# A hybrid decoder layer on one core: LayerNorm, pointwise convolution and a quarter of the first half of the output projection placed inside the prompt's stick-breaking attention

## The chip, the core and the metric

One core of a Trainium2 chip runs the whole program in one launch. The metric is the device time of one execution in microseconds, lower is better. Engines are named as the profile names them: PE (TensorE matmuls), PEld (its weight loads), DVE (VectorE), ACT (ScalarE), POOL (GpSimd), SP (SyncE, which here only issues DMAs).

## What is computed

One layer of a decoder trunk, for a prompt of 2048 tokens and for 32 sample tokens (8 sequences of 4). The parts that matter here:

```python
z = rms_norm(x) @ w_in                       # split into the inputs and gates of four groups
y_c = silu(layer_norm(depthwise_conv(u))) @ w_pw + b_pw     # group A, 512 channels
y_p = per_group_linear(causal_mean(u) - u) * scale          # group B (pooling), 512 channels
y_s = stick_breaking_attention(q, k, v)      # group C, 8 heads x 64, strictly causal
y_m = cross_attention(mq, mem)               # group D, 4 heads x 128
mix = concat(y_c*silu(cg), y_p*silu(pg), y_s*silu(sg), y_m*silu(mg))   # 2048 channels
out = x + rms_norm(mix @ w_out)              # w_out is 2048 x 1024
y   = rms_norm(out)
# attention of one head: z = q.k/8 + bias, beta = sigmoid(z), gamma = sigmoid(-z)
# a[q,k] = beta[q,k] * product of gamma[q,j] over the keys j between k and q
```

## The kernel before, in words

Everything is float32; a matmul that has to be exact splits both factors into a rounded float32r part and a remainder (names ending in `hi` and `lo`) and sums three products, hi·hi, hi·lo, lo·hi. Intermediate results that a later stage reads go through DRAM: `mixd` holds the gated outputs of all four groups, 16 blocks of 128 channels by 2080 tokens (blocks 0 to 3 convolution, 4 to 7 pooling, 8 to 11 attention, 12 to 15 cross-attention).

The program has three stages one after the other. Instructions on PE stand in the order in which the code issues them; the other engines' instructions are put into an order by a scheduler when the program is built, and each engine works through its own queue in that order.

1. **Projection and sample attention** (about the first 1516 us): `z`, the depthwise convolution, pooling, cross-attention and the 32 sample tokens' attention over the paged cache. The change doesn't touch it.

2. **The prompt's attention**, generator `sb_prompt` (L1158), 16 blocks (4 head pairs by 4 blocks of 512 queries), each going over its key blocks from the diagonal back to the first. A *step* is one call of `score` (L1183): four matmuls into a PSUM tile `S` of two banks (L1189), two sigmoids on ACT (`gam` L1195, `be` L1197), then, two steps late, on DVE a `tensor_tensor_scan` along the keys that forms the running product `E` (L1209; L1206 on the diagonal), and on POOL the product `be*E` (L1222). Six steps later `turn` (L1227) transposes `be` on PE into a PSUM tile with tag `AT` of which there are two (L1233), which DVE or ACT copies out (L1237 on the diagonal; elsewhere every third on DVE, L1243, the others on ACT, L1241); two steps after that `values` (L1246) multiplies with V into `av` (L1253). The scan takes `max(gamma*previous, data1)`, where `data1` is 0, or on the diagonal 0 with a triangle of 1; that tile, `ZM` (L1165), fills one PSUM bank, and every scan reads from it. PSUM is full: `S` twice two banks, `AT` twice one, `av` one, `ZM` one.

   `sb_prompt` yields twice per step with a cost; the loop around it (L1633 on) spends that cost on other work: first `side_work` (cross-attention of the sample tokens, the end of their attention, five tiles of `w_out`), and from the 300th yield of some 340 on `conv_work`, one piece per yield.

   `conv_post` (L1310) is that other work: LayerNorm, swish and pointwise convolution of group A, in eight blocks of 256 tokens. Per block: sums over channels on POOL, `center` (mean by a matmul with ones, L1334; four subtractions on DVE, L1337; squares on ACT, L1339), `scale` (variance by matmul, L1345; square root on ACT, L1347; reciprocal, L1348, and eight more operations on DVE, L1353 and L1357; sigmoids on ACT, L1356), `point` (four times twelve matmuls of 256 columns, L1374, gated and biased on DVE, L1377, and stored to `mixd`).

3. **The output projection.** For each of 17 token tiles (16 of the prompt, one of the samples) and each half `hf` of 512 output columns, 16 channel blocks by three products: 48 matmuls of 512 columns (L1619; 32 for the samples). `out_mix` (L1438) loads 8 channel blocks of `mixd` and splits them (ACT L1451, DVE L1453); `out_weights` (L1415) loads and splits `w_out`. `order` (L1599) lists half-tiles; those that hold the convolution's channels (half 0) come five tiles after the others, and the rest of `conv_post` (all but its first block) and the weights of the second half run between the matmuls of the first half. `out_keep` (L1458) copies the first half's results to `okeep` and sums their squares; `out_tile` (L1464) finishes a tile in the second half.

## Time and profile before

| | us |
|---|---|
| median of 3 runs | 2501.28 (2498.33 to 2506.47) |
| the profiled execution's own time | 2494.88 |
| its span, first to last instruction | 2493.2 |
| mean granted PE clock in it | 0.983 |
| first score matmul of the prompt's attention | 1516.4 |
| last matmul of it begins | 2046.2 |

The span and all times inside it come from one profiled execution. A row of the profile such as `L1209 DVE TENSOR_TENSOR_SCAN E<-gam,cr,ZM ... x192 | 235.8, 1267 | 5.5` is a group of instructions: source line, engine, operation, output and inputs by their names in the program, shapes, how many; then us busy in all, mean ns of one; then us for which the engine stood idle just before them, and what ended that. PE's matmuls are pipelined: an instruction's recorded length is longer than the distance to the next one, so PE's cost is read from starts or from counts per time, not from its busy share.

### The profile page before, as it was taken

To read this page: it belongs to the slowest core of one execution; us is meant where nothing else is said; L and a number is where in the kernel's file an instruction comes from. 1 tells how busy PE (TensorE), PEld (TensorE's weight loads), DVE (VectorE), ACT (ScalarE), POOL (GpSimd) and SP (SyncE) were. 2 spreads that over 40 slices of the span, in tenths; PEclk is the share of its full clock that TensorE was granted. 3 is DMA by queue.
4 is the path that set the end of the run, shared out by engine and by line. 5 is a ranking of instruction groups with operands and counts; after the bars stand their busy time and mean duration, and the time that the engine had idled before them with its cause. 6 is when DMAs were issued, how large, how long until landed. Compare 5 with 4: busy or idle time off the path is not lost. (4 is left out here: it accounts for less than half of the span.)

```text
span 2493.2 us, 42024 instructions
## 1 busy us (share of the span) xinstructions
PE 2331.7 (94%) x16154; PEld 1812.5 (73%) x16154; DVE 1695.1 (68%) x2402; ACT 1073.9 (43%) x1867; POOL 1231.6 (49%) x1330
## 2 busy tenths in 40 slices
PE   6998999999999999999999997898999879999998
PEld 6997878788888677777777774455555547887786
DVE  5442495969747663587877677899899966554554
ACT  5324224242442322223232343777888854444443
POOL 2543545455564555645555663567766742320221
PEclk9999999999999999999999998999999999999999
DMA  5688677777778899878877748434332116445664
GB/s 178 216 273 285 240 259 263 239 258 256 259 246 303 286 345 326 298 267 277 286 265 273 266 167 211 128 86 111 98 85 74 46 45 180 138 117 149 179 193 140
DMA packets 347554, 518.07 MB, mean 208 GB/s; under 512 B 26257, under 2 KB 250897, under 8 KB 330954
## 3 DMA queue, kind: packets, MB, share of 16 engines
q1 hardware_dynamic: 291978, 246.67, 33.4%
q0 software_dynamic: 55376, 268.72, 30.5%
q8 instruction: 127, 2.08, 0.3%
q14 instruction: 73, 0.60, 0.1%
HBM read 444.12 MB, written 71.81 MB: 207 GB/s over the span
## 5 line engine op out<-in xcount | busy, mean ns | idle before, releaser
L856 DVE STREAM_TRANSPOSE T<-kt 128x1024 f32<-128x1024 f32 x256 | 309.1, 1226 | 193.4 <-PE sSA L869 179.3
L823 POOL DMA_INDIRECT vt<-in_cache_v_dram,idv x256 | 250.8, 980 | 241.3 <-PE sO L908 179.5
L519 DVE SCALAR_TENSOR_TENSOR cacc<-U,par,cacc 128x512 f32<-128x512 f32 x480 | 358.9, 748 | 8.0
L1222 POOL TENSOR_TENSOR be<-be,E 128x512 f32<-128x512 f32 (+2 forms) x320 | 304.8, 955 | 117.8 <-DVE E L1209 64.6
L1209 DVE TENSOR_TENSOR_SCAN E<-gam,cr,ZM 128x513 f32<-128x513 f32 x192 | 235.8, 1267 | 5.5 <-POOL be L1222 4.1
L823 POOL DMA_INDIRECT kt<-in_cache_k_dram,idk x128 | 125.5, 981 | 228.1 <-DVE T L856 169.6
L1233 PEld LDWEIGHTS AT<-ident,be 128*128 128x128 f32 x1088 | 118.3, 142 | 158.4 <-DVE at L1243 27.7
L1619 PE MATMUL acc<-wohi,mh 128*128 128x512 f32 (+1 forms) x544 | 219.8, 404 | 6.6 <-ACT wohi L1432 6.6
L1619 PE MATMUL acc<-wolo,mh 128*128 128x512 f32 (+1 forms) x544 | 216.2, 397 | 0.0
L1195 ACT ACTIVATE gam<-S,nbias_bc 128x128 f32<-128x128 f32 (+1 forms) x224 | 177.3, 792 | 83.0 <-PE S L1189 48.4
L1619 PE MATMUL acc<-wohi,ml 128*128 128x512 f32 x512 | 203.5, 398 | 0.0
L1233 PE MATMUL AT<-ident,be 128*128 128x128 f32 x1088 | 163.8, 285 | 38.5 <-DVE at L1243 23.2
L1197 ACT ACTIVATE be<-S,bias_bc 128x128 f32<-128x128 f32 (+1 forms) x224 | 176.6, 788 | 0.0
L1189 PE MATMUL S<-kT,Q 128*128 128x512 f32 (+3 forms) x640 | 172.1, 392 | 1.5 <-DVE sg1sg L611 1.5
L1253 PE MATMUL av<-at,V 128*64 128x512 f32 (+3 forms) x640 | 154.9, 563 | 2.1 <-DVE sbo L1258 2.1
L869 PE MATMUL sSA<-T,W 128*32 128x128 f32 x4096 | 139.5, 277 | 14.1 <-DVE T L856 12.9
L1453 DVE TENSOR_TENSOR ml<-mr,mh 128x1024 fp32r<-128x1024 f32 (+1 forms) x65 | 82.8, 1274 | 95.8 <-ACT mh L1451 95.7
L869 PEld LDWEIGHTS sSA<-T,W 128*32 128x32 f32 x4096 | 105.0, 110 | 51.6 <-issue 45.5
L1483 POOL TENSOR_TENSOR oxt<-oxt,oy 128x1024 f32<-128x1024 f32 (+1 forms) x16 | 39.3, 2457 | 183.4 <-DVE oy L1478 162.6
L1619 PEld LDWEIGHTS acc<-wohi,mh 128*128 128x128 f32 (+1 forms) x544 | 101.9, 187 | 31.7 <-ACT wohi L1432 8.2
L908 PE MATMUL sO<-vt,saT 128*32 128x512 f32 x1024 | 122.0, 593 | 0.0
L1619 PEld LDWEIGHTS acc<-wolo,mh 128*128 128x128 f32 (+1 forms) x544 | 101.8, 187 | 24.8 <-DVE wolo L1433 0.9
(560 smaller groups left out, 6002.3 us busy)
## 6 DMA issues: line engine op xcount, KB each, us to landing
mr<-mixd SPq DMA_DIRECT2D x63, 512.0 KB
Q<-qd SPq DMA_DIRECT2D x64, 256.0 KB
xtp<-in_x_prompt_dram SPq DMA_DIRECT2D x16, 512.0 KB
kT<-kd SPq DMA_DIRECT2D x64, 128.0 KB
wor<-in_w_out_dram SPq DMA_DIRECT2D x32, 256.0 KB
oxt<-in_x_prompt_dram SPq DMA_DIRECT2D x16, 512.0 KB
out_dram<-oy SPq DMA_DIRECT2D x15, 512.0 KB
wr0mem<-in_w_mem_kv_dram SPq DMA_DIRECT2D x8, 512.0 KB
```

The source lines that it names most:

```text
L519: dve.scalar_tensor_tensor(out=ps, in0=U[:, a + k : a + k + H], scalar=wd[:, k : k + 1], in1=ps, op0=ALU.mult, op1=ALU.add)
L823: pool.indirect_dma_start(out=dst, out_offset=None, in_=rows, in_offset=bass.IndirectOffsetOnAxis(ap=idx, axis=0))
L856: dve.transpose(T[:, 2 * hh : 2 * hh + 2].rearrange("p s j t -> p (s j t)"), kt[:, 2 * hh : 2 * hh + 2].rearrange("p s j d -> p (s j d)"))
L869: pe.matmul(sSs[n][32 * g : 32 * g + 32, P * ml : P * (ml + 1)], lhsT=W[:, jj, :], rhs=T[:, :, jj, :], start=i == 0, stop=i == 3, tile_pos ...
L1189: pe.matmul(S[:, j, :n], lhsT=Q[hh][:, x, P * (q2 + j) : P * (q2 + j + 1)], rhs=KT[hp, hh, kc][:, :n], start=x == 0, stop=x == 1)
L1195: act.activation(out=ga[:, j0:j1, 512 - n : 512], in_=S[:, j0:j1, :n], func=AF.Sigmoid, bias=nbias_bc[:, h : h + 1], scale=-1.0)
L1197: act.activation(out=be[:, j0:j1, :n], in_=S[:, j0:j1, :n], func=AF.Sigmoid, bias=bias_bc[:, h : h + 1])
L1209: dve.tensor_tensor_scan(out=E[:, j][:, ::-1], data0=ga[:, j][:, ::-1], data1=ZM[:, 0:1].to_broadcast([P, 513]), initial=carry[hh, q2][:, ...
L1222: pool.tensor_tensor(out=be[:, j, :m], in0=be[:, j, :m], in1=E[:, j, 513 - n : 513 - n + m], op=ALU.mult)
L1233: pe.transpose(ap_[:, P * qt : P * (qt + 1)], A[hp, qb, kc, hh, qt][:, P * r : P * (r + 1)], ident)
L1253: pe.matmul(av[64 * hh : 64 * hh + 64, c], lhsT=V[:, 4 * kc + r, 64 * hh : 64 * hh + 64], rhs=ats.pop((hp, qb, kc, r, hh))[:, c], start=dg ...
L1619: pe.matmul(o[:rows], lhsT=m[i][:, k, :rows], rhs=W[hf, 8 * half + k][w], start=n0 + k == 0 and i == w == 0, stop=n0 + k == 15 and (i if t ...
```

## The change

- The tile of zeros and triangle shrinks to 129 columns of its PSUM bank (`ZX`), and columns 256 to 511 of the same bank become an accumulator. A scan on the diagonal that is longer than 128 becomes two: 128 columns with the triangle, then the rest with a zero that is broadcast and the first scan's last value as its start.
- `conv_post` becomes part of the side work: it follows the samples' work at once and is paced by the attention's cost (one piece per 1.25 units of it; the attention has about 362).
- New generator `early_out`, one piece per 4.2 units: for all 17 token tiles the pooling blocks 4 to 7 are multiplied with the first 512 output columns, in two passes of 256 columns, each pass twelve matmuls in two groups of six into the shared bank, then a copy on ACT; the result goes to DRAM (`okd`). Then it loads weights 8 to 11.
- The output stage works in quarters (4 channel blocks): three per tile in the first half, four in the second. `okeep` is filled from `okd` and the first half's sums are added to it. The weights of the second half are spread over the matmuls of the first; the queue of prepared tiles is five quarters of 256 KB instead of four halves of 512 KB; eight accumulators instead of six.

```diff
-PACE = 2.5
-OPACE = 1.15
-LAG = 5
+PACE = 1.6
+CPACE = 1.25
+EPACE = 4.2
+WPACE = 9.0
+SLATE = 8
+LAG = 3
-D1 = 6
-D2 = 12
-CSTART = 300
+D1 = 4
+D2 = 8
...
-        ZM = bps.tile([P, 512], F32, name="ZM", bufs=1)
-        act.copy(ZM, zm)
+        act.copy(ZX[:, : P + 1], zm)
+        zero = lambda n: ZX[:, 0:1].to_broadcast([P, n])
...
-                        dve.tensor_tensor_scan(out=E[:, j, 512 - n : 512][:, ::-1], data0=ga[:, j, 512 - n : 512][:, ::-1],
-                                               data1=ZM[:, 512 - n : 512][:, ::-1], initial=1.0, op0=ALU.mult, op1=ALU.max)
+                        dve.tensor_tensor_scan(out=E[:, j, 384:512][:, ::-1], data0=ga[:, j, 384:512][:, ::-1],
+                                               data1=ZX[:, 1 : P + 1][:, ::-1], initial=1.0, op0=ALU.mult, op1=ALU.max)
+                        if n > P:
+                            dve.tensor_tensor_scan(out=E[:, j, 512 - n : 384][:, ::-1],
+                                                   data0=ga[:, j, 512 - n : 384][:, ::-1], data1=zero(n - P),
+                                                   initial=E[:, j, 384:385], op0=ALU.mult, op1=ALU.max)
...
+    def out_products(o, hf, t, g, m, cols, first, last):
+        rows = P if t < 16 else 2 * NS
+        for k in range(4):
+            for i, w in ((0, 0), (0, 1), (1, 0)) if t < 16 else ((0, 0), (0, 1)):
+                pe.matmul(o[:rows], lhsT=m[i][:, k, :rows], rhs=W[hf, 4 * g + k][w][:, cols],
+                          start=first and k == i == w == 0, stop=last and k == 3 and (i if t < 16 else w) == 1)
+            yield
+    def early_out():
+        yield from out_weights(0, range(4, 8), opm, pool, True)
+        o = ZX[:, 256:512]
+        mix = {0: out_mix(0, 1, "e", pool)}
+        for t in range(17):
+            if t < 16:
+                mix[t + 1] = out_mix(t + 1, 1, "e", pool)
+            m = mix.pop(t)
+            rows = P if t < 16 else NS
+            ke = opm.tile([P, 512], F32, tag="ke", name=f"ke{t}", bufs=1)
+            for q in range(2):
+                cols = slice(256 * q, 256 * q + 256)
+                for k, _ in enumerate(out_products(o, 0, t, 1, m, cols, True, True)):
+                    if k % 2:
+                        yield
+                if t < 16:
+                    act.copy(ke[:, cols], o)
...
+            wq.dma_start(okd[t, :rows], ke[:rows])
+        yield
+        yield from out_weights(0, range(8, 12), opm, pool, True)
     def out_keep(t, o):
-        act.activation(out=okeep[:rows, t], in_=o[:rows], func=AF.Square, accum_out=ssk[:rows, t : t + 1])
-        dve.tensor_copy(okeep[:rows, t], o[:rows])
+        dve.tensor_tensor(out=okeep[:rows, t], in0=o[:rows], in1=okeep[:rows, t], op=ALU.add)
+        sq = op.tile([P, 512], BF16, tag="oksq", name=f"oksq{t}", bufs=1)
+        act.activation(out=sq[:rows], in_=okeep[:rows, t], func=AF.Square, accum_out=ssk[:rows, t : t + 1])
...
-    order = [(0, t, 1) for t in range(LAG)]
+    order = [(0, t, 2) for t in range(LAG)]
     for t in range(17):
-        order += [(0, t, 0)] + [(0, t + LAG, 1)] * (t + LAG < 17)
-    order += [(1, t, h) for t in [0, 1, 2, 16, *range(3, 16)] for h in range(2)]
+        order += [(0, t, 3), (0, t, 0)] + [(0, t + LAG, 2)] * (t + LAG < 17)
+    order += [(1, t, g) for t in [0, 1, 2, 16, *range(3, 16)] for g in range(4)]
...
+        if steps > SLATE:
+            sdue -= cost
+            while side is not None and sdue <= 0.0:
+                    sdue += next(side)
...
+        edue -= cost
+        while early is not None and edue <= 0.0:
+            edue += EPACE
+                next(early)
...
-    wts = out_weights(0, [*range(8 + NPRE, 16), *range(8)], lambda k: opw)
+    wts = out_weights(0, [*range(12, 16), *range(4)], opw, dve)
```

More of the change, by code (lines that the diff above doesn't have):

```diff
@@ L53 @@
 X0 = 8
-PACE0 = 1.5
 SEND = 0.97
@@ new lines, with prepare @@
+    order += [(1, t, g) for t in [0, 1, 2, 16, *range(3, 16)] for g in range(4)]
+    left_ = {}
+    for x in order:
+        left_[x[:2]] = left_.get(x[:2], 0) + 1
+    total_ = dict(left_)
+    mix, accs = {}, {}
+    def prepare(i):
+        for x in order[: i + 1]:
+            if x not in mix:
+                mix[x] = out_mix(x[1], x[2], f"{x[0]}_", dve if op else pool)
+                if x[0] == 0 and x[2] == 0:
+                    rows = P if x[1] < 16 else NS
+                    sp.dma_start(okeep[:rows, x[1]], okd[x[1], :rows])
@@ L1654 @@
-    for _ in side or ():
-        pass
-    bx.close()
-    for _ in range(early, NPRE):
-        next(first)
+                early = None
+        if "last" in flags and side is None and early is None:
+            if lead is None:
+                os_.close()
+                accp = oy.enter_context(tc.tile_pool(name="oacc", bufs=1, space=PSUM, side="left", reuse_waits="tile"))
+                prepare(1)
+                lead = out_part(order[0])
+            next(lead, None)
+    for g_ in (side, early):
+        for _ in g_ or ():
+            pass
@@ L1660 @@
+    bx.close()
+    if lead is None:
+        os_.close()
+        accp = oy.enter_context(tc.tile_pool(name="oacc", bufs=1, space=PSUM, side="left", reuse_waits="tile"))
+        prepare(1)
+        lead = out_part(order[0])
+    for _ in lead:
+        pass
     op = oy.enter_context(tc.tile_pool(name="op", bufs=2, side="right", reuse_waits="tile"))
[L1661 to L1662 removed]
@@ L1689 @@
-    other = other_work()
-    due, ope = 0.0, None
+    w1 = out_weights(1, range(16), op2, dve)
+    ope = None
+    due = 0.0
     for i, x in enumerate(order):
-        hf, t, half = x
+        hf = x[0]
         if hf and ope is None:
-            while "weights" not in flags:
-                next(other, 0)
+            for _ in w1:
+                pass
             ow.close()
```

191 lines of the change are left out of this document (71 added, 120 removed).

## The prediction

> **What bounds the kernel now.** I read the page first, then the busy times of three stretches, then the groups of instructions in them, then the waits.
>
> ```profile
> PE 2331.7 (94%) x16154; PEld 1812.5 (73%) x16154; DVE 1695.1 (68%) x2402; ACT 1073.9 (43%) x1867; POOL 1231.6 (49%) x1330
> ...
> PE acc L1619 14%; PE cz L1374 2%; DMA mr<-mixd 1%; PE av L1253 0%; PE AT L1233 0%; POOL slo L1359 0%; DMA mixd<-sbo 0%; DMA cgt<-gcd 0%; PE cm L1334 0%; PE cv L1345 0%; ACT mh L1451 0%; DVE cgt L1377 0%; PE S L1189 0%; ACT csg L1356 0%; DVE ml L1453 0%
> ```
>
> PE is 94% busy over the span, and the chain that ended last is made of the output projection's matmuls (`acc`). It only reaches back into the last fifth of the span, so it says nothing of the attention. The second view takes the span apart: body and drain of the prompt's attention, head and body of the output projection, then one head pair with side work, one without, and 100 us of nothing but output matmuls.
>
> ```profile
> core 0: us, PE busy (x) PEld busy (x) DVE busy (x) ACT busy (x) POOL busy (x), PEclk, DMA share, GB/s
> 1534.60:2018.30 483.70, 430.92 (x2447) 248.02 (x2443) 438.25 (x575) 375.83 (x571) 326.66 (x469) 0.99 0.34 90
> 2018.30:2047.00 28.70, 23.99 (x117) 12.39 (x115) 15.25 (x24) 15.43 (x28) 9.57 (x12) 0.94 0.08 23
> 2047.00:2070.00 23.00, 16.61 (x70) 12.94 (x71) 11.25 (x15) 8.74 (x12) 0.65 (x1) 0.78 0.59 177
> 2070.00:2482.90 412.90, 408.51 (x1927) 336.19 (x1926) 214.98 (x314) 172.33 (x316) 97.61 (x80) 1.00 0.54 158
> 1659.30:1786.40 127.10, 112.29 (x631) 65.05 (x630) 113.68 (x153) 99.89 (x156) 88.76 (x125) 0.97 0.37 99
> 1786.40:1902.70 116.30, 107.41 (x595) 61.77 (x594) 106.22 (x134) 95.42 (x146) 80.84 (x118) 0.99 0.33 84
> 2300.00:2400.00 100.00, 100.00 (x437) 80.10 (x436) 54.51 (x76) 40.84 (x76) 20.94 (x9) 1.00 0.63 188
> ```
>
> Columns after the length: PE, PEld, DVE, ACT, POOL busy, granted clock, DMA share, GB/s. Two stages have different limits. In the output projection's body PE is busy for 408.51 of 412.9 us and DVE for 215: PE is the bound, and what is taken off PE there comes off the time. In the attention's body DVE is busy for 438.25 of 483.7 us (91%). PE shows 430.92, but its records overlap, so that is not its need; the waits show who waits for whom in 400 us of it:
>
> ```profile
> PEld AT L1233 <- DVE at L1243: 26.6, 16, 3.8
> PEld AT L1233 <- DVE at L1237: 26.4, 39, 1.8
> ...
> DVE at L1243 <- PE AT L1233: 12.8, 12, 2.4
> ...
> DVE E L1206 <- ACT gam L1195: 8.7, 11, 1.3
> ```
>
> PE waited 53 us in these two rows alone for DVE to empty the transposes' PSUM tiles, and DVE 21.5 us in the other two for PE and ACT. So DVE is the bound of the attention and PE has room, but they are close and coupled through two PSUM tiles. The head pair without side work shows the same: 106.22 us of DVE in 116.30 us.
>
> **The change part by part.** The profiled execution took 2494.88 us, its span 2493.2 with 1.7 around it; the median of the runs shown, 2501.28, is 6.4 above it. I make the sum against the profile and add the difference to the median.
>
> *Off the output projection: pooling's matmuls.* 16 tiles x 4 blocks x 3 products plus 8 for the samples are 200 of the 1600 matmuls of 512 columns. The last stretch holds 437 in 100 us, 0.229 us each: 200 x 0.229 = -45.8 us. The first quarter runs in the attention's drain as fifteen matmuls did before. `okd` puts back as many bytes as the pooling quarters took (17 x 256 KB either way); the stage moved 158 GB/s before, and the convolution's loads leave it, so I count that at nothing. If it weren't hidden, it would show as PE waiting for `okeep`'s addition.
>
> *Off it: the pointwise matmuls.* One of the 32 bursts, from its first start to the start of what follows:
>
> ```profile
> 2120.06 0.28 PE L1374 MATMUL cz<-shi,pwhi 128*128 128x256 f32 x1
> ...
> 2121.36 0.28 PE L1374 MATMUL cz<-shi,pwlo 128*128 128x256 f32 x1
> 2121.48 0.40 PE L1619 MATMUL acc<-wohi,mh 128*128 128x512 f32 x1
> ```
>
> 2121.48 - 2120.06 = 1.42 us for twelve, 0.118 us each; 32 x 1.42 = -45.4 us. Together -91 us, which has to be found in a stage where PE is the bound, and PE had no other reason to wait there for more than 4.4 us in 412.9.
>
> *Head of the output projection.* Before, PE did 70 matmuls (16 us at 0.229) in the 23 us from 2047 to 2070: 7 us lost. Now eight weight tiles and four quarters must be there within the first 48 matmuls (11 us), some 3 MB, which at the 177 GB/s of that row take 17 us: 6 us lost. I take no difference; the bounds are 7 us gained (nothing lost any more) and 10 lost (all 17 us waited for).
>
> *Into the attention: the convolution's work on DVE.* The groups that ran between the output matmuls:
>
> ```profile
> L1377 DVE SCALAR_TENSOR_TENSOR cgt<-cz,par,cgt 128x256 f32<-128x256 f32 (+1 forms) x32 | 15.5, 486 | 42.3 <-PE cz L1374 33.3 <-DMA cgt<-gcd 9.1
> L1357 DVE SCALAR_TENSOR_TENSOR cy<-cy,par,csg 128x256 f32<-128x256 f32 (+1 forms) x28 | 14.1, 557 | 3.8 <-ACT csg L1356 3.8
> L1353 DVE SCALAR_TENSOR_TENSOR cy<-cy,par,crs 128x256 f32<-128x256 f32 (+1 forms) x28 | 13.8, 554 | 0.0
> ...
> L1348 DVE RECIPROCAL crs<-crs 128x256 f32<-128x256 f32 (+1 forms) x7 | 12.5, 1781 | 7.9 <-ACT crs L1347 7.9
> ...
> L1337 DVE TENSOR_TENSOR cy<-cy,cm 128x256 f32<-128x256 f32 (+1 forms) x24 | 8.8, 421 | 2.0 <-PE cm L1334 2.0
> ```
>
> 15.5 + 14.1 + 13.8 + 12.5 + 8.8 = 64.7 us. They cost nothing there, because DVE had 198 us free; in the attention's body it has 45.4. Priced at one us for one us, with DVE's idle time as it is: +64.7 us.
>
> *Into the attention: the split scans.* Of 128 diagonal scans 96 are longer than 128 columns and become two.
>
> ```profile
> L1209 DVE TENSOR_TENSOR_SCAN E<-gam,cr,ZM 128x513 f32<-128x513 f32 x192 | 235.8, 1267 | 5.5 <-POOL be L1222 4.1 <-POOL cr L1218 0.7 <-ACT gam L1195 0.6
> L1243 DVE COPY at<-AT 128x512 f32<-128x512 f32 x64 | 43.3, 676 | 23.3 <-PE AT L1233 22.8
> L1206 DVE TENSOR_TENSOR_SCAN E<-gam,ZM 128x512 f32<-128x512 f32 x32 | 38.6, 1208 | 0.3
> ...
> L1206 DVE TENSOR_TENSOR_SCAN E<-gam,ZM 128x128 f32<-128x128 f32 x32 | 13.0, 407 | 6.1 <-ACT ZM L1166 4.6 <-ACT gam L1195 1.3
> ```
>
> From 128 to 512 columns a scan grows by 801 ns, 2.09 per column, so 140 ns are fixed. The 513-column scan, which starts from a value in a tile as the second part does, is 57 ns above that line. 96 x 0.197 = +19 us (+13 with a constant's start, the lower bound).
>
> *The matmuls in the attention, and the new wait.* PE gets 400 matmuls of 256 columns for pooling (400 x 0.118 = 47 us) and the 45.4 us of bursts. By its recorded busy time that is 523 us, DVE's is 522 (438 + 84): PE as full as DVE. They hide as long as PE's room of the two wait rows and more is there. But the accumulator shares its bank with the zeros that every scan reads. In the built program of the changed kernel, 68 scans carry a wait on PE, one after each of the 68 groups of six matmuls, and each of the 34 copies out of the bank waits on DVE. Behind a waiting scan stands everything on DVE, and for DVE wait POOL's product, then PE's transposes. One group is 6 x 0.118 = 0.71 us, so the price lies between nothing and 68 x 0.71 = 48 us. In that order 60 of the 68 scans have other DVE work between them and the scan before, a copy of 0.68 us for instance, and 8 have none (6 us). I take 19, nearer to the low end.
>
> The Trainium skill speaks against this placing: "PSUM — Partial Sum Buffer", section "PSUM bank collisions raise a hardware error", says that two engines may not touch one bank in the same partitions at the same time, even at different columns, and tells to guard by bank. That would mean that no scan and no pooling group ever overlap, as the order's waits also have it; no trace of before shows it, since `ZM` was read by DVE alone, and the 48 us above would be its bound.
>
> *ACT and POOL.*
>
> ```profile
> L1356 ACT ACTIVATE csg<-cy,par 128x256 f32<-128x256 f32 (+1 forms) x28 | 12.4, 503 | 0.1
> L1358 ACT CAST shi<-cy 128x256 fp32r<-128x256 f32 (+1 forms) x28 | 10.2, 405 | 3.4 <-DVE cy L1357 3.3
> ...
> L1347 ACT ACT_TABLE_LOAD x7 | 9.0, 1283 | 0.1
> L1356 ACT ACT_TABLE_LOAD x7 | 9.0, 1283 | 5.3 <-DVE cy L1353 5.3
> L1339 ACT ACTIVATE csq<-cy 128x256 f32<-128x256 f32 (+1 forms) x24 | 8.3, 409 | 0.0
> ```
>
> ```profile
> L1433 POOL TENSOR_TENSOR wolo<-wor,wohi 128x512 fp32r<-128x512 f32 x5 | 6.4, 1278 | 0.0
> ```
>
> These rows hold 49 us that move, among them fourteen table loads of 1.28 us. Pooling adds 17 casts of 512 and 34 copies of 256 columns; at 0.405 us for 256 and at most twice that for 512, 28 us. On 375.83 us in a body that is some 100 us longer that is 453 of 584, 78%. On POOL the whole of the output body's 97.61 us is more than what moves, and 17 remainders at 1.28 add 22: at most 446, 76%. I count both at nothing, covered by that idle time; uncovered, a POOL instruction ahead of `be` would hold up a transpose by up to 1.28 us each time. The samples' work is 1.6 instead of 2.5 units apart and ends earlier, its amount is the same. SP's loads of Q and K now stand behind stores of `okd` and `mixd` that wait for ACT and DVE; a step's loads are issued a block ahead, so nothing.
>
> **Sum.** -91 + 0 + 64.7 + 19 + 19 = +12 us: 2494.9 + 12 = 2507 in the terms of the profile, 2513 in those of the median.
>
> **The rivals.**
>
> *Faster: the convolution fills DVE's gaps.* One mechanism, in the attention's body: DVE's 45.4 us of waits are filled, because the scheduler can put independent work where the scan or the copy would wait. For it: the waits of the third view are for PE and ACT, and work that waits for neither now stands in the queue. Against it: PE has less room than before. With half of the gaps filled (-23) and the scans' waits covered (-19), 12 - 42 = -30: 2471. It decides as soon as more than 12 us, a quarter of the gaps, is filled.
>
> *Slower: the coupling costs more than the work.* The two head pairs measure a marginal price: with side work 127.10 us and 113.68 of DVE, without 116.30 and 106.22. 10.8 us of time for 7.5 of DVE, 1.45. At that price the 84 us of DVE work cost 38 more: +50, 2551. Against it: part of that side work is small chains that wait for DMAs.
>
> *It doesn't do what it says.* If loads in quarters of 256 KB held up PE in the output projection, the 91 us would not all come off; a third left there gives +42, 2543. For it, four load tiles now serve mix, weights and `okeep`'s neighbours; against it, 188 GB/s went beside a PE at 100 of 100 us in the last row.
>
> **How the numbers follow.** My forecast, the sum with its terms off by some 20 us to either side, has 0.42; the faster rival 0.33, the coupled one 0.18, the last 0.07. About 0.3% (7.5 us) is what a measurement of this kernel can tell from no change. Of the forecast's 0.42, 0.03 lies below -7.5, 0.12 inside, 0.27 above. Faster: 0.33 + 0.03 = 0.36. Same: 0.12. Slower: 0.27 + 0.18 + 0.07 = 0.52. Cases of both signs hold much of the chance; the forecast's own range is 2493 to 2533. Low end of the whole: half the gaps filled (-23), no scan's wait (-19), the scans' lower bound (-6), a hidden head (-6): 12 - 54 = -42, 2459. High end: the scans' waits whole (48 instead of 19, +29) and half of the marginal price (+19): +60, 2561.
>
> **What would show it.** In the changed kernel's profile: the last attention matmul near 2150 instead of 2047, and some 355 us from there to the end instead of 446; DVE near 90% in the attention's body; scans waiting for `ZX` matmuls with about 0.3 us each; pointwise bursts still 1.42 us. The forecast is wrong if the attention grows by less than 85 us with DVE well above 92% busy (the faster rival), if DVE falls under 87% while PE or ACT are waited for (the coupled one), or if PE is under 97% busy in the output projection's body (the last).

## The result and the profile after

| | before | after |
|---|---|---|
| median of four runs each | 2500.02 (2498.33 to 2506.47) | 2613.77 (2610.31 to 2615.34) |
| ratio, 95% interval | | 1.0448 (1.0426 to 1.0470) |
| span of the profiled execution | 2493.2 | 2608.6 |
| attention: first score matmul to the start of the last `av` matmul | 1516.4 to 2046.2: 529.8 | 1519.1 to 2269.2: 750.1 |
| from there to the end | 447.0 | 339.4 |

The kernel became 114 us slower where 12 were forecast. The output stage gave 108 us back, more than the 91 forecast. The attention took 220 us instead of 103. So the whole miss lies in the attention.

The page of the kernel after, engines and chain of waits:

```profile
PE 2373.3 (91%) x16354; PEld 1846.0 (71%) x16354; DVE 1712.0 (66%) x2545; ACT 1099.3 (42%) x1968; POOL 1250.4 (48%) x1352
...
PE 58%; DVE 18%; issue 6%; DMA 5%; ACT 5%; POOL 3%; SPq 1%; DVEq 0%; ACTq 0%; POOLq 0%
PE acc L1460 12%; DVE cacc L518 4%; DVE E L1212 4%; PE sSA L868 3%; PE sO L907 3%; PE S L1188 3%; PE AT L1236 2%; PE av L1256 2%; DVE T L855 2%; PE z1ca L221 2%; PE z1cb L221 2%; PE z1mg L221 2%; PE z1q L221 2%; PE z1v L221 2%; PE z0ca L221 2%
```

The chain now runs back through the whole program with `E`, `S`, `AT` and `av` in it. Before, it reached back no further than the last 32 us of the attention. The share of each engine fell: nobody is fuller than before, and yet the span grew. The busy times of five stretches (columns as in the prediction: length, PE, PEld, DVE, ACT, POOL, granted clock, DMA share, GB/s): the attention while other work runs in it, the third head pair, the 59 us after all other work has ended, head and body of the output stage:

```profile
1534.00:2190.00 656.00, 520.28 (x2987) 344.24 (x2988) 476.13 (x730) 409.72 (x676) 365.01 (x514) 0.92 0.36 99
1900.70:2099.80 199.10, 158.45 (x892) 106.33 (x890) 147.22 (x223) 130.04 (x220) 117.28 (x163) 0.91 0.31 86
2189.80:2248.40 58.60, 53.20 (x286) 30.38 (x284) 54.30 (x70) 46.87 (x63) 41.82 (x57) 0.97 0.06 19
2269.20:2290.00 20.80, 16.51 (x57) 10.63 (x54) 9.80 (x15) 8.62 (x15) 0.65 (x1) 0.92 0.79 245
2290.00:2598.00 308.00, 308.00 (x1337) 247.90 (x1335) 146.49 (x243) 123.94 (x261) 43.56 (x16) 1.00 0.58 172
```

Read the second row against its twin of before (116.30 us, DVE 106.22, clock 0.99). The same head pair takes 199.10 us, of which DVE is busy 147.22, 74% instead of 91%. PE, ACT and POOL have idle time too, and the clock is at 0.91. In the third row, with no other work left, DVE is at 93% and the pace is the old one. The output stage's body has PE at 308.00 of 308.00 us: that side of the forecast held.

The groups with most idle time ahead of them, and the waits of 400 us of the attention (who waited, for whom, us in total, times, longest):

```profile
L1225 POOL TENSOR_TENSOR be<-be,E 128x512 f32<-128x512 f32 x192 | 209.6, 1096 | 152.8 <-DVE E L1212 142.5 <-ACT at L1244 3.7 <-ACT gam L1194 2.2
...
L1194 ACT ACTIVATE gam<-S,nbias_bc 128x1024 f32<-128x1024 f32 x96 | 107.5, 1119 | 110.8 <-PE S L1188 85.9 <-issue 18.0 <-ACT be L1196 5.0
...
L1460 PE MATMUL ZX<-wohi,mhe 128*128 128x256 f32 x128 | 43.8, 342 | 36.8 <-ACT ke L1481 28.5 <-DVE E L1212 6.2 <-DVE E L1208 2.1
...
L1212 DVE TENSOR_TENSOR_SCAN E<-gam,cr,ZX 128x513 f32<-128x513 f32 x192 | 235.1, 1267 | 40.3 <-PE ZX L1460 26.5 <-ACT gam L1194 6.7 <-ACT be L1196 2.5
```

```profile
ACT gam L1194 <- PE S L1188: 73.4, 39, 6.4
DVE cgt L1380 <- PE cz L1377: 31.7, 17, 3.5
...
DVE E L1212 <- PE ZX L1460: 17.8, 17, 3.1
PE ZX L1460 <- ACT ke L1481: 17.7, 8, 6.6
ACT ke L1481 <- DVE E L1212: 17.1, 7, 5.0
...
PE cz L1377 <- DVE at L1240: 11.9, 9, 2.6
```

The row for `gam` of the kernel before:

```profile
L1195 ACT ACTIVATE gam<-S,nbias_bc 128x1024 f32<-128x1024 f32 x96 | 107.9, 1124 | 57.2 <-PE S L1189 23.7 <-issue 20.7 <-ACT be L1197 11.8
```

Its idle time went from 57.2 to 110.8 us, and the part for `S` from 23.7 to 85.9: ACT waits for PE. Three waits form a ring: the pooling matmuls (`ZX`) wait for the copy `ke` on ACT, the copy waits for a scan on DVE, and the scan waits for pooling matmuls. Two of its links in the timeline (start, length, engine, line, operation, and in brackets the idle time before it and what ended that):

```profile
1938.04 0.39 PE L1460 MATMUL ZX<-wohi,mhe 128*128 128x256 f32 x1 [1.10 <-DVE E L1208]
...
1939.16 2.46 DVE L1212 TENSOR_TENSOR_SCAN E<-gam,cr,ZX 128x513 f32<-128x513 f32 x2 [1.17 <-ACT be L1196]
...
1941.70 0.37 ACT L1481 COPY ke<-ZX 128x256 f32<-128x256 f32 x1 [2.05 <-DVE E L1212]
...
1941.85 0.54 PE L1377 MATMUL cz<-shi,pwhi 128*128 128x256 f32 x1 [1.67 <-DVE at L1240]
...
1942.19 0.42 PE L1377 MATMUL cz<-slo,pwhi 128*128 128x256 f32 x1
...
1942.41 0.42 PE L1377 MATMUL cz<-shi,pwlo 128*128 128x256 f32 x1
```

PE stood 1.10 us until a scan had let go of the bank. Two scans then ran, behind a wait of 1.17 us (for a sigmoid, by the row), and the copy of 0.37 us waited 2.05 us for them. PE meanwhile stood 1.67 us for a transposes' tile. Then its burst ran at half rate: 0.22 us from start to start instead of 0.118. This is the only one of the 32 bursts that did so throughout. The median burst took 1.53 us to the start of what follows, near the 1.42 forecast.

Over the whole attention the scans waited 42 times for pooling groups, 46 us in all:

```profile
DVE E L1212 <- PE ZX L1460: 26.5, 27, 3.3
DVE E L1205 <- PE ZX L1460: 19.7, 15, 2.4
```

That is 1.1 us each, where the prediction had 68 waits of about 0.3. And the chain of waits, taken over the 656 us of the first stretch alone, holds the moved matmuls (shares of those 656 us by line; the view breaks off at its end):

```profile
by line: DVE E L1212 12.1%; PE S L1188 9.0%; issue 8.9%; PE AT L1236 7.3%; PE av L1256 7.3%; PE ZX L1460 6.8%; PE cz L1377 6.5%; ACT gam L1194 4.6%; DVE at L1240 3.7%; ACT be L1196 3.4%; ACT at L1244 2.2%; DVE E L1208 1.8%; DVE at L1246 1.7
```

6.8% are 45 us of pooling's matmuls and 6.5% are 43 us of the bursts, about all that the prediction counted of them (47 and 45 us) and put at nothing.

### The profile page after: what moved, and what is told of

Same layout as the page of the kernel before. It is cut to its first block, busy times and chain, and to the rows that moved or that the text cites. A ratio compares the mean times of both kernels' runs of the same rounds, so it can differ in the third digit from the quotient of the medians.

```text
span 2608.6 us, 42918 instructions
## 1 busy us (share of the span) xinstructions
PE 2373.3 (91%) x16354; PEld 1846.0 (71%) x16354; DVE 1712.0 (66%) x2545; ACT 1099.3 (42%) x1968; POOL 1250.4 (48%) x1352
## 4 chain that ended last, share of the span: by engine, by line
PE 58%; DVE 18%; issue 6%; DMA 5%; ACT 5%; POOL 3%; SPq 1%; DVEq 0%; ACTq 0%; POOLq 0%
PE acc L1460 12%; DVE cacc L518 4%; DVE E L1212 4%; PE sSA L868 3%; PE sO L907 3%; PE S L1188 3%; PE AT L1236 2%; PE av L1256 2%; DVE T L855 2%; PE z1ca L221 2%; PE z1cb L221 2%; PE z1mg L221 2%; PE z1q L221 2%; PE z1v L221 2%; PE z0ca L221 2%
## 5 line engine op out<-in xcount | busy, mean ns | idle before, releaser
L1212 DVE TENSOR_TENSOR_SCAN E<-gam,cr,ZX 128x513 f32<-128x513 f32 x192 | 235.1, 1267 | 40.3 <-PE ZX L1460 26.5
L1460 PE MATMUL acc<-wohi,mh 128*128 128x512 f32 (+1 forms) x476 | 189.2, 397 | 3.8 <-ACT mh L1449 2.5
L1460 PE MATMUL acc<-wolo,mh 128*128 128x512 f32 (+1 forms) x476 | 187.3, 394 | 0.5 <-DVE wolo L1434 0.5
L1188 PE MATMUL S<-kT,Q 128*128 128x512 f32 (+3 forms) x640 | 177.9, 404 | 10.6 <-ACT be L1196 9.2
L1460 PE MATMUL acc<-wohi,ml 128*128 128x512 f32 x448 | 177.4, 396 | 0.0
L1256 PE MATMUL av<-at,V 128*64 128x512 f32 (+3 forms) x640 | 160.7, 581 | 0.6 <-DVE sbo L1261 0.6
L1188 PEld LDWEIGHTS S<-kT,Q 128*128 128x128 f32 x640 | 113.5, 207 | 23.3 <-ACT be L1196 10.2
L1452 DVE TENSOR_TENSOR ml<-mr,mh 128x512 fp32r<-128x512 f32 x110 | 78.4, 723 | 54.9 <-ACT mh L1449 54.4
L1449 ACT CAST mh<-mr 128x512 fp32r<-128x512 f32 (+1 forms) x119 | 69.9, 599 | 93.8 <-PE acc L1460 67.6
```

What stands on the lines that cost most here:

```text
L1188: pe.matmul(S[:, j, :n], lhsT=Q[hh][:, x, P * (q2 + j) : P * (q2 + j + 1)], rhs=KT[hp, hh, kc][:, :n], start=x == 0, stop=x == 1)
L1212: dve.tensor_tensor_scan(out=E[:, j][:, ::-1], data0=ga[:, j][:, ::-1], data1=zero(513), initial=carry[hh, q2][:, j, :], op0=ALU.mult, op1 ...
L1256: pe.matmul(av[64 * hh : 64 * hh + 64, c], lhsT=V[:, 4 * kc + r, 64 * hh : 64 * hh + 64], rhs=ats.pop((hp, qb, kc, r, hh))[:, c], start=dg ...
L1460: pe.matmul(o[:rows], lhsT=m[i][:, k, :rows], rhs=W[hf, 4 * g + k][w][:, cols], start=first and k == i == w == 0, stop=last and k == 3 and ...
```

## The experiments

The length of the attention is measured as in the table above. It comes from one profiled execution of each kernel. The stretch behind it runs the same code in the kernel before and in the eight runs made from that kernel, and took 443 to 449 us in these nine; so differences of up to 5 us count as none. In the edits shown, `...` and short names such as `scr` (a scratch tile) stand for what is left out. Four theories stood against each other: the **shared bank** (turns between scans, pooling groups and copies), the **transposes' tiles** (the convolution's means, variances and bursts take them), **lumps** (PE gets more at once than a step can absorb), and the **work itself** (so many us of it, by the prediction's prices).

### Each part alone

Convolution held until the attention is over, then run alone:

```diff
-            for _ in conv_post(cp, side_ps):
-                yield CPACE
+    def conv_work():
+        with tc.tile_pool(name="cp", bufs=1, side="left", reuse_waits="tile") as cp:
+            yield from conv_post(cp, side_ps)
...
-    for g_ in (side, early):
+    for g_ in (side, early, conv_work()):
```

> The changed kernel, but the convolution's generator is held until the attention is over and then run alone, so that the attention holds the pooling products, the shared bank and the split scans, and no LayerNorm or pointwise work. Read from it: the attention's length, from the first score matmul to the start of the last av matmul (530 us before, 750 changed). If the shared bank is the main cost, most of the 220 us stay: 670 us or more. If the convolution's work in the transposes' two PSUM tiles is the main cost, 600 us or less. If each part costs its own work on DVE and nothing else: 530 + 19 for the split scans + 19 for the waits = 568 us. The total is not to be compared, since the convolution then runs with nothing beside it.

Measured: attention 635.1 us (2651.51 in all, with the convolution alone at the end).

No pooling products:

```diff
-        yield from out_weights(0, range(4, 8), opm, pool, True)
...
-            m = mix.pop(t)
...
-                for k, _ in enumerate(out_products(o, 0, t, 1, m, cols, True, True)):
...
-            wq.dma_start(okd[t, :rows], ke[:rows])
...
-                    sp.dma_start(okeep[:rows, x[1]], okd[x[1], :rows])
+                    sp.dma_start(okeep[:rows, x[1]], xp[...])
```

> The changed kernel without the pooling products: the early half of pooling is neither loaded, multiplied nor copied, and the first half's result starts from rows of the input in place of it (so that part of the output is left out); the bank is then read by the scans alone. The convolution stays in the attention. If the shared bank is the main cost, the attention shrinks from 750 to 640 us or less. If the convolution in the transposes' tiles is, it stays at 690 us or more. By the sum on record, 530 + 65 + 19 = 614 us.

Measured: 652.5 us (2512.28 in all).

Neither of the two, with both edits together (the control):

> The control: the changed kernel with the convolution held until after the attention and without the pooling products (left out as in the run without pooling), so that the split, the new pace of the samples' work and the early weights alone remain. All theories: about 538 us of attention, as with the split alone. If the pace of the samples' work or its place costs, more, and the two parts cost less by as much.

Measured: 525.5 us, 13 less than expected. The control holds nothing of the convolution's LayerNorm, while the kernel before had its first block in the attention (some 10 us of DVE more, and 10 of ACT), which may be the 13; no run shows it apart. The new pace of the samples' work shows no cost. Against this control pooling costs 635.1 - 525.5 = 110 us and the convolution, now all eight blocks of it, 652.5 - 525.5 = 127, together 12 more than the 225 between the control and the changed kernel. No single theory names one culprit: both parts cost far more than the prediction's price (19 and 65 us). Neither of them pays alone either, since each takes some 46 us of matmuls out of the output stage.

### The split scans

```diff
-  dve.tensor_tensor_scan(out=E[:, j, 512 - n : 512][:, ::-1], ..., data1=ZM[:, 512 - n : 512][:, ::-1], initial=1.0, ...)
+  dve.tensor_tensor_scan(out=E[:, j, 384:512][:, ::-1], ..., data1=ZM[:, 384:512][:, ::-1], initial=1.0, ...)
+  if n > P:
+      dve.tensor_tensor_scan(out=E[:, j, 512 - n : 384][:, ::-1], ..., data1=ZM[:, 0:1].to_broadcast([P, n - P]),
+                             initial=E[:, j, 384:385], ...)
```

> The kernel before with nothing changed but the split of the 96 longer diagonal scans. The sum on record prices it at 19 us (13 to 19): attention 530 to about 549 us, total near 2520. If the split lies beside waits of DVE: 530 to 540 us.

Measured: 538.3 us, +8.5 (2500.81 beside 2494.78). DVE's work grew as forecast, by 0.2 us per split (404 + 1013 ns for what was 1208), 20 us in all. Less than half of it shows.

### What work costs that nobody waits for

Doubled score matmuls, copies that nobody reads, and both, in the kernel before:

```diff
+                if not dg:
+                    pe.matmul(S[:, j, :n], lhsT=Q[hh][:, 0, ...], rhs=KT[hp, hh, kc][:, :n], start=True, stop=True)
...
+                if not dg:
+                    dve.tensor_copy(scr, ZM)
```

> The kernel before with 192 score matmuls of 512 columns done twice (the same result is written again): 192 x 0.229 = 44 us of PE in the attention that bring no new wait, tile or transfer, about what the pointwise bursts (45) or the pooling products (47) are. As the prediction counted PE, hidden beside DVE: 530 us stay, 540 at most. If PE has no room in the attention: 530 + 44 = 574 us.

> The kernel before with 96 copies on DVE of 512 columns from PSUM to a tile that nobody reads: 96 x 0.68 = 65 us of DVE in the attention that wait for nothing and for which nobody waits, as much as the convolution has there. One us for one us, as on record: 530 + 65 = 595. If they fill DVE's gaps: 550 to 575. At the coupled rival's 1.45: 624.

> Both additions of the two runs above in one kernel: 44 us of PE and 65 of DVE, without any new wait between engines. If work on the two engines lies side by side, the attention is as long as with the costlier of the two alone, about 595 to 605. If PE and DVE take turns, whatever is added to either adds up: 530 + 44 + 65 = 640.

Measured: 546.5 us with 44 us of PE (+17), 552.5 with 64 us of DVE (+23), 566.1 with both (+36).

```profile
L1213 DVE COPY scr<-ZM 128x512 f32<-128x512 f32 x96 | 64.1, 668 | 0.0
```

A us of free work costs 0.35 to 0.38 us, on either engine, and the two nearly add up. So the gaps of both engines can be filled, to nearly two thirds: the mechanism of the prediction's faster rival exists. But 108 us of such work cost 36, and the change's work cost 220. So the amount of the work is not what sets its cost.

### Lumps

The same 192 matmuls in 32 lumps of six, in the kernel before:

```diff
+                for _ in range(3 if kc == 0 and qb > 1 else 0):
+                    pe.matmul(S[:, j, :n], ..., start=True, stop=True)
```

> The kernel before with the same 192 doubled matmuls of 512 columns as in the run with extra matmuls (44 us of PE, there +16.7 us of attention, two in each of 96 steps), but in 32 lumps of six (1.37 us, as long as a pointwise burst), in four steps in a row as the pointwise bursts are. No tile, wait or transfer is added. If PE's additions cost what a step can't absorb (a step of about 2.9 us leaves PE some 0.5 us), the lumps cost more than spread work: +30 us or more. If what costs in the changed kernel is the waits between engines and not when PE has its work: +17 us as before.

Measured: 555.5 us, +26 instead of +17.

And the convolution's bursts further apart, in the run without pooling:

```diff
-D1 = 4
-D2 = 8
+D1 = 8
+D2 = 0
...
                 wq.dma_start(mixd[co, :, a0:a1], g[:, :N])
                 yield
                 yield
+                yield
...
-            yield from point(i)
+            for co, _ in enumerate(point(i)):
+                if co == 3 and i + 1 < len(blocks):
+                    center(i + 1)
+                yield
```

> The run without pooling (attention 652.5 us) with the pointwise bursts three pieces apart instead of two (one in 1.4 steps instead of one in each step), and the next block's centering between them. Work, tiles and waits are the same. If the lumps of PE work are what costs: 635 us or less. If it is the number of round trips through the two transposes' tiles, or DVE's work: 645 us or more.

Measured: 645.7 us, 7 less than 652.5. Lumps cost something: in lumps, free matmuls cost 0.59 us per us instead of 0.38. They don't bring the price to one us for one us, and spreading the bursts saves little.

### The convolution taken apart

In the run without pooling, a copy in place of the root, and one product of twelve per burst:

```diff
-            act.activation(out=rs[:, :N], in_=vps[:, :N], func=AF.Sqrt, bias=eps_t)
+            act.copy(rs[:, :N], vps[:, :N])
...
-                    for w, x in ((whi, shi), (whi, slo), (wlo, shi)):
+                pe.matmul(ps[:, :N], lhsT=whi[...], rhs=slo[...], start=True, stop=True)
```

> The run without pooling again (attention 652.5 us there) and a copy in place of the square root on ACT (the root of the variance is left out, so outputs of the convolution differ). It takes 16 table loads of 1.28 us, 21 us of ACT, out of the attention and changes nothing on PE and DVE. If ACT's table loads hold up gam and with it DVE, the attention shrinks by 20 us or more; if ACT has room as the prediction counted, by less than 5 us.

> The run without pooling again (652.5 us) with one of the twelve pointwise matmuls per output block (eleven are left out): the bursts shrink from 1.42 to 0.12 us, the tiles, waits and all work of DVE, ACT and POOL stay. If PE's bursts cost their own time, the attention shrinks by about 32 x 1.3 = 42 us; if PE hides them as the prediction counted, by less than 10 us, and DVE's work or the two tiles are what costs.

Measured: 647.3 us without the root (-5, no more than what counts as none), 618.7 with one product (-34 for 42 us of matmuls). ACT's 16 table loads are nearly covered, as the prediction had it. PE's matmuls are not: here they cost 0.8 us per us, where free matmuls cost 0.38, or 0.59 in lumps.

Empty turns of a transposes' tile, as many as the convolution makes, in the kernel before:

```diff
+            if not dg and q2:
+                tt = bps.tile([P, 512], F32, tag="AT", name=f"tt{nm}", bufs=2)
+                pe.transpose(tt[:, :P], ident, ident)
+                dve.tensor_copy(scr, tt[:, :8])
```

> The kernel before with 48 empty turns of a transposes' PSUM tile, as many as the convolution's means, variances and bursts make: one transpose of 128 columns (0.11 us) into the tile, one copy of 8 columns out of it by DVE, nobody uses the result. About 5 us of PE and 5 to 10 of DVE. If the turns are what costs in the changed kernel (127 us for the convolution, of which 34 were the bursts' matmuls and 23 to 65 are DVE's work, so 0.5 to 1.5 us a turn): 530 + 25 to 70 us of attention. If not: 540 at most.

Measured: 531.9 us, +2 (2498.12 beside 2504.59).

```profile
L1203 PE MATMUL tt<-ident 128*128 128x128 f32 x48 | 14.6, 304 | 8.5 <-DVE at L1242 5.3 <-ACT at L1246 1.7 <-DVE at L1248 1.1
```

A tile that is taken and given back at once costs next to nothing. The theory of the transposes' tiles falls for the convolution. Of its 127 us, 34 are the bursts' matmuls, 5 the table loads, and 88 remain for 72 us of DVE, 42 of ACT (`csg` 14.4, `shi` 12.4, `csq` 11.3, `crs` 3.8) and 61 of POOL. Three of their rows, on POOL in the run without pooling:

```profile
L1362 POOL TENSOR_TENSOR slo<-cy,shi 128x256 fp32r<-128x256 f32 x28 | 21.7, 792 | 27.6 <-ACT shi L1361 27.6
...
L1310 POOL TENSOR_TENSOR csq<-csq,csq 128x256 f32<-128x256 f32 x7 | 5.1, 731 | 0.2
...
L1309 POOL TENSOR_TENSOR cs<-cy 128x256 f32<-128x256 f32 x7 | 5.1, 729 | 3.3 <-issue 2.1 <-DMA mixd<-cgt 1.2
```

With four more groups like the last two, and the wider last block (3.6, and six times 0.8), these are the 61 us of POOL. `slo` stands 27.6 us waiting for ACT, and behind it stands `be`, for which the transposes wait. That speaks for chains that cross four queues, each in its order. No run took ACT's or POOL's part away, so these 88 us are not taken apart.

### Pooling taken apart

With the convolution held: two products of twelve, groups of three, and an accumulator in a transposes' tile.

```diff
-                for k, _ in enumerate(out_products(o, 0, t, 1, m, cols, True, True)):
-                    if k % 2:
-                        yield
+                for k in range(2):
+                    pe.matmul(o, lhsT=m[0][:, 2 * k], rhs=W[0, 4 + 2 * k][0][:, cols], start=k == 0, stop=k == 1)
+                    yield
```

```diff
-EPACE = 4.2
+EPACE = 2.1
...
-                    if k % 2:
-                        yield
+                    yield
```

```diff
-        o = ZX[:, 256:512]
...
+                o = side_ps(f"eo{t}_{q}")[:, :256]
```

> The run with the convolution held (attention 635 us) with two of the twelve pooling products per pass (ten are left out, so that half of pooling's result is partial): groups of one matmul instead of six, 40 us less of PE; loads, splits, copies, the shared bank and its turns between scans, groups and copies stay. If pooling costs its own matmul time: 595 us or less. If it costs the round trips of the shared bank, whatever the size of a group: 620 us or more.

> The run with the convolution held (attention 635 us) with the pooling matmuls in groups of three, twice as often, instead of groups of six. If lumps on PE are what costs: shorter, 620 us or less. If it is the turns in the shared bank (each group must wait for a scan and a scan for a group, whatever its size): longer, 645 us or more.

> The first run again (convolution held until the attention is over; attention 635 us there), with one difference: the pooling groups accumulate in one of the two transposes' PSUM tiles instead of beside the zeros. No scan waits for PE and no copy for a scan any more, but each pass holds a transposes' tile. If the waits of the shared bank are what pooling costs (61 us of scans behind PE groups in that run), the attention is about 575 us. If it is pooling's matmuls, copies and loads themselves, it stays near 635 us, or grows if the two tiles are the tighter place.

Measured: 600.2 us with two products, -35 for 40 us of matmuls; 660.9 with groups of three, +26; 658.5 in a transposes' tile, +23. The first two agree: the matmuls cost nearly their own time (0.87), and each of the 68 additional turns costs another 0.38 us, against what lumps would do. The third doesn't answer its question: no scan waited for PE any more, but a pass held one of two tiles over two pieces of the plan, and the transposes waited for the other one:

```profile
PEld AT L1236 <- DVE at L1240: 38.1, 35, 2.5
...
PE AT L1236 <- DVE at L1240: 31.1, 27, 2.3
...
PEld AT L1236 <- ACT at L1244: 21.9, 19, 1.5
```

In the first run, with pooling in the bank, the first of these rows had 11.2 us. So that run moved the wait, and doesn't show what the bank costs. Empty turns come nearer to it, in the kernel before with the split scans:

```diff
+            if not dg and (hh, q2) != (1, 2) and (hh or q2 or kc % 2):
+                pe.transpose(ZM[:, P : 2 * P], ident, ident)
+                if q2 == 0:
+                    act.copy(scr, ZM[:, P : P + 8])
```

> The kernel before with the split scans (attention 538 us) and 56 empty turns of the zeros' bank: one transpose of 128 columns into unused columns of the bank, and after 32 of them a copy of 8 columns out by ACT. About 6 us of PE and 6 of ACT. If the turns in the bank are what pooling costs (110 us, of which 35 were matmuls; 26 us more for 68 more groups): 538 + 20 to 75 us of attention. If the bank's turns cost only their own time: 550 at most.

Measured: 606.5 us beside 538.3, +68 for 12 us of work (2569.04 in all). Two places of its timeline:

```profile
1800.82 0.30 PE L1202 MATMUL ZM<-ident 128*128 128x128 f32 x1 [2.14 <-DVE E L1219]
...
1801.23 2.45 DVE L1219 TENSOR_TENSOR_SCAN E<-gam,cr,ZM 128x513 f32<-128x513 f32 x2 [0.56 <-PE ZM L1202]
...
1806.42 0.17 ACT L1204 COPY scr<-ZM 128x8 f32<-128x8 f32 x1
...
1806.69 4.80 DVE L1219 TENSOR_TENSOR_SCAN E<-gam,cr,ZM 128x513 f32<-128x513 f32 x4 [2.63 <-ACT scr L1204]
...
1808.05 1.09 POOL L1232 TENSOR_TENSOR be<-be,E 128x512 f32<-128x512 f32 x1 [3.08 <-DVE E L1219]
...
1809.24 1.12 ACT L1195 ACTIVATE gam<-S,nbias_bc 128x1024 f32<-128x1024 f32 x1 [1.68 <-DVE E L1219]
...
1812.13 1.09 PE L1243 MATMUL AT<-ident,be 128*128 128x128 f32 x8 [1.43 <-DVE at L1253]
```

A matmul of 0.30 us stands on PE behind a scan (2.14 us), and ahead of all of PE's other work. The scan after it waits 0.56 us. The copy of 0.17 us stands on ACT behind the sigmoids, and a scan waits 2.63 us for it. Then four scans run one after the other, `be` on POOL waits 3.08 us for the first, `gam` 1.68 us for its buffer, and PE 1.43 us for a copy on DVE that stands behind them. So 56 turns cost 1.2 us each, the 32 copies included. In sum that is as much as pooling leaves beside its matmuls: 110 - 41 (0.87 of its 47 us) = 69.

Two things keep this from being pooling's price. The waits are others: here `gam` stands mostly for scans, to have its buffer back, while in the changed kernel it stood mostly for `S`:

```profile
L1195 ACT ACTIVATE gam<-S,nbias_bc 128x1024 f32<-128x1024 f32 x96 | 107.7, 1122 | 121.2 <-DVE E L1219 66.0 <-PE S L1189 33.0 <-DVE E L1214 6.1
```

And groups of three, which add turns of PE but no copies, cost 0.38 us a turn, not 1.2. At 0.38 the 68 groups are 26 of the 69 us, and 43 are left for the 34 copies and all else. That is an estimate from these runs; no run left out the copies, or pooling's splits on ACT and POOL.

### The bank without sharing

Zeros and triangle in SBUF, in the changed kernel and in the one before:

```diff
-        act.copy(ZX[:, : P + 1], zm)
-        zero = lambda n: ZX[:, 0:1].to_broadcast([P, n])
+        zero = lambda n: zm[:, 0:1].to_broadcast([P, n])
```

> The changed kernel with one difference: the scans read their zeros and the triangle from a tile in SBUF, so that the pooling accumulator has the bank to itself and no scan waits for PE, and no copy out of the bank for a scan. If the shared bank is the main cost, the attention shrinks from 750 to about 640 us or less, and the whole kernel from 2614 to 2510 or less. If the convolution is, the attention stays at 710 us or more. A scan that reads zeros from SBUF may itself have another length: read it from its row (1267 ns before for 513 columns).

> The kernel before with the zeros and the triangle in SBUF instead of in PSUM, the control for the previous run. All theories: if the scan's length doesn't depend on where its zeros are, no change (2500 us, attention 530 us, 513 columns in 1267 ns). If SBUF costs more per scan, 320 scans grow by that much and the attention with them, one us for one us or a little more.

Measured: 792.7 and 655.5 us (2656.09 and 2619.09 in all). Scan and product in the kernel before and with zeros in SBUF:

```profile
L1222 POOL TENSOR_TENSOR be<-be,E 128x512 f32<-128x512 f32 x192 | 209.1, 1091 | 92.9 <-DVE E L1209 64.6 <-ACT be L1197 7.8 <-PE AT L1233 7.4
```

```profile
L1207 DVE TENSOR_TENSOR_SCAN E<-gam,cr,zm 128x513 f32<-128x513 f32 x192 | 322.6, 1717 | 12.6 <-POOL be L1220 9.1 <-issue 2.2 <-POOL cr L1214 1.2
...
L1220 POOL TENSOR_TENSOR be<-be,E 128x512 f32<-128x512 f32 x192 | 294.0, 1550 | 71.2 <-DVE E L1207 49.7 <-PE AT L1231 10.4 <-ACT at L1239 4.2
```

The scan grew from 1267 to 1717 ns, and POOL's product from 1091 to 1550, without a change of its own. That spoils the direct reading. The pair can be subtracted: with no shared bank, the change costs 792.7 - 655.5 = 137 us of attention instead of 220, which leaves 83 for the bank. But the pair isn't clean: in the changed kernel with zeros in SBUF the scan took 1605 ns on average, not 1717, which is 21 us less in 192 scans. At one us for one us the bank's part would be 62. So it is some 60 to 83 us by this way.

## Why the prediction was wrong, point by point

- **Bound before, output stage.** Right. PE is busy for 308.00 of 308.00 us there, and the stage gave 107.6 us. The sum's 91.2 were matmuls alone; 4.4 were idle time of PE in the body of before, 2.3 of the head (4.3 instead of 6.6 us without a matmul). The remaining 9.7 aren't attributed: that the stage gave more than forecast is luck.
- **Split scans, +19.** The work was right (20 us), its price too high: +8.5.
- **DVE's idle time as it is, one us for one us.** Wrong for free work, which costs 0.35, and wrong the other way for the convolution, whose parts beside the matmuls cost 93 us. The 65 were DVE's work, seven of eight blocks of LayerNorm; all eight have 72, and ACT's and POOL's parts lie in the 93 too.
- **PE's matmuls at nothing.** This step failed, and it is the largest: 34 us of 42 and 35 of 40 were measured, so 34 + 41 = 75 us by the runs for a term of nothing. PE's room was misread. The two rows of 53 us that the prediction took for PE's waits are those of its weight loads (PEld). The matmuls themselves waited half as long in the same 400 us of the kernel before:

```profile
PE AT L1233 <- DVE at L1243: 22.3, 20, 3.6
...
PE AT L1233 <- DVE at L1237: 4.6, 8, 1.1
```

That is 27 us against 92 us of matmuls that were to be hidden. Free matmuls still found room for 27 of their 44 us. Why the moved ones found less isn't shown in full; lumps explain a part (0.59 instead of 0.38).

- **The scans' waits in the shared bank, +19 between 0 and 48.** This step failed too, since it left the right value, some 60 to 80 us, out of its bounds. It took one group's length, 0.71 us, as the most that a turn could cost. The scans' own waits were 1.1 us each, 46 us in all; an empty turn with 0.11 us of PE cost 1.2 us, copies included. The copies, which the prediction names, got no price. The timelines show what a turn waits for beside the guest's length: a place in three queues (group behind scan, copy behind scan and sigmoids, scan behind copy), and all that stands behind each of them waits as well. How the 69 us divide between groups and copies stays open. The page that the prediction named, "PSUM — Partial Sum Buffer" of the Trainium skill, section "PSUM bank collisions raise a hardware error", says that such accesses must be kept apart; the trace agrees in that scans and groups never overlapped in the rows shown. The 48 us derived from it were the prediction's own.
- **ACT and POOL at nothing.** Table loads: right within what one execution shows (5 us of 21). For the rest the runs can't tell; part of the 88 us above lies there.
- **The rivals.** The coupled one named the sign that came (DVE under 87% while PE and ACT are waited for; it is 74%), but priced it at 1.45 us per us of DVE from two head pairs; 220 us for 84 of DVE are 2.6. Those pairs held work in small chains with few matmuls and no shared bank, so their price couldn't show either. The faster one failed: free work did fill gaps (27 of 44 us on PE, 41 of 64 on DVE), but the convolution, which waits for other engines and is waited for, didn't. The last one didn't come: the output stage gave what was forecast, and more.

By the runs: 525.5 (control, split included) + 41 and 69 (pooling: matmuls, bank and copies) + 34 + 5 + 88 (convolution: matmuls, table loads, the rest) = 762, 12 more than the 750 measured.

## What to carry to other kernels

Before work is moved into a stage that isn't bound by one full engine but by engines that wait for each other, put free work of the same size into it (a repeated matmul, a copy that nobody reads) and an empty turn through each buffer that the work would share: the first gave 0.35 us per us here, the second next to nothing for a tile of its own and 1.2 us, copies included, for a bank that another engine's running instruction reads. Read an engine's room from its own rows: PE's weight loads stood twice as long as its matmuls. A guest in a PSUM bank is priced by the queues at whose heads it and its neighbours wait, not by its own length. When every engine's busy share falls and the span grows, look for a ring of waits, not for the fullest engine.

## What the runs showed of the hardware that wasn't expected

- **A scan with a second operand in SBUF.** 1717 ns instead of 1267 for 513 columns, and POOL's products beside it 1550 instead of 1091. The Trainium skill's page "SBUF — State Buffer", section "🔬 SBUF: two separate sides", says that DVE with two SBUF inputs and a reading GpSimd take turns on one port pair, whole instructions at a time; the trace agrees in that both grew by 0.45 us on average, and not evenly: of the 192 scans 54 stayed under 1.3 us and 77 took 2.0 or more, and of the 192 products 84 stayed under 1.12 us and 97 took 1.8 or more. The tile of zeros in PSUM is thus worth 116 us here (2619.09 beside 2502.83), and the bank that it holds is what the change shared.
- **The clock.** The granted clock was 0.91 in the changed attention's third head pair against 0.99 before. One of the 32 bursts ran at half rate throughout, after PE had stood for 1.67 us, and so did six of the 64 pooling groups of six. The first product of pooling, 342 ns on average in the row above, has a median of 283, near the 282 of the bursts before: most matmuls kept their recorded length. What the lower clock adds to the 220 us was not separated by any run.
